# Five changes of order in one layer of a hybrid encoder: tables, scales, maxima, low halves and residual transposes

## Chip, cores and metric

The kernel runs on one core of one Trainium2 chip, in one launch. The metric is the device time of one execution in microseconds (us), the median of three runs.

## What is computed

One encoder layer over 2048 tokens of width 1024:

- h = RMSNorm(x), then one combined projection h @ w_in; its columns are q, k and v of mixer A (8 heads of 64) and the latents of mixer B (c_q of 256, c_kv of 128, a rotary key of 32).
- Mixer A is dilated sliding-window attention in three patterns, (window, stride) = (128, 1), (512, 4) and (2048, 16), with a relative bias per head; the three outputs are merged by their softmax denominators.
- Mixer B is latent attention: q = rmsnorm(c_q) @ w_q_up, keys and values = rmsnorm(c_kv) @ w_kv_up, a rotary part of 32 for q and one rotary key for all heads, and a softmax over all 2048 keys in 8 heads of 96 (values of 64).
- x = x + concat(rmsnorm(A), rmsnorm(B)) @ w_out.
- A router picks one of 4 groups of experts and 2 of 8 experts in it for each token; the gated MLPs (1024 to 256 to 1024) are added to x. A final RMSNorm follows.

```
sc = (qn . kn + qr . kr) * 96 ** -0.5       # mixer B, per head
o  = softmax(sc) @ v
x  = x + concat(rmsnorm(out_a), rmsnorm(out_b)) @ w_out
```

All inputs and outputs are float32. Where the kernel multiplies in float16 or in the rounded form of float32, it splits an operand into a high and a low part and adds three products (hi hi, hi lo, lo hi).

## The kernel before

The kernel is written as a sequence of stages, in the order in which they run: the combined projection (until about 427 us of the span), mixer A (427 to 700), the preparation of mixer B (706 to 770), its main loop (to 1515), the output projection with the router (to 1797), the experts (to about 2300) and the final norm. Every engine has its own queue and takes its instructions in the order in which the program issues them (manual_schedule, no planner); engines meet through semaphores, which follow from tiles and from the number of buffers of a pool. A tile of a pool with two buffers waits for the last reader of the tile before the last.

**Mixer A** works through 160 units (8 heads, 20 units: 4 with the table of stride 16, 8 with that of stride 1, 8 with that of stride 4). The bias tables t16, t1 and t4 are loaded once; scale_tables (L570) has POOL multiply the part of one pair of heads by a scale. For the first pair it is called ahead of the loop (L582), for the others at unit 12 of an odd head. A step s of the loop (L756) issues, in this order: the permutations of q, the scores of unit s on PE (qk), the bias and row minimum on DVE (soft1), POOL's subtraction of unit s-1 (soft2, L676), ACT's exponential of unit s-2 (soft3, L697), PE's transposes of unit s-3, and the low part and the product with v of units s-4 and s-5.

**The preparation of mixer B** (mla_prep, L1006) goes through 16 tiles c of 128 tokens: ACT normalises the latents (stage_a1, two tiles ahead); PE transposes them, ACT and DVE split them into high and low parts (stage_a2, one tile ahead); PE multiplies with the weights of q and v, DVE and POOL make the rotary part, ACT and DVE write the values VB (stage_b). qprep transposes q of head 0, put_q (ACT, DVE) writes its high and low parts Qh and Ql each fourth tile; krows and kprep make the keys of head 0. All transposes of it and krows, kprep and qk_scales take their PSUM tiles from the pool tag pT, which has two buffers. qk_scales (L793) is one small matmul and 17 operations of DVE on a few columns that set the scales of q and k; it stands ahead of stage_a2(0).

**The main loop of mixer B** (mla, L821) has 256 steps s: 8 heads, 4 blocks of 512 queries (index m counts the 32 pairs), 8 pairs of key tiles. A step issues the scores of two key tiles (6 matmuls), two exponentials of ACT (hi in float16 and p32), the low part lo = p32 - hi of the step before (lows, L920: DVE makes columns 0 to LV of each 512, POOL the rest, LV = 256), and, each second step, the products with VB of two earlier steps (pv). Two maximum passes per step (maxpass, L874: one matmul of 128 queries against 512 keys, one maximum of DVE over the row, and after the fourth of a row group a maximum over the four) are made for a block to come: they lead by 20 passes, and these 20 stand ahead of the loop, followed by mrow(0), which transposes the maxima and writes them as a row of Qh. From head 7 on, parts of the output projection are mixed into the steps (ahead5).

**The output projection** (loop over n at L1826) handles 16 tiles of 128 tokens. In an iteration n, proj(n) is a generator of the 32 matmuls and their sums, which are issued in chunks (ahead, some); between the chunks stand the work on other tiles. After chunks 1 and 2, trans(n+1) has PE transpose the merged and scaled rows ab of the next tile (8 transposes L1368, the copies to mT_hi on ACT, mT_lo on DVE). After chunks 3 and 4, trans2(n-1) has PE transpose the new residual rows x of the tile before (8 transposes, L1437), which resid(n-1) (DVE, L1395) has written after proj(n-1). Both use the pool tag pT of that stage.

Of the kernel before, what the change touches and what calls it, by code (L numbers as in the profile page):

```python
# [36 lines left out]
class K:  # L37
# [475 lines left out]
    def phase3(self):  # L513
        nc, tc, io, dr = self.nc, self.tc, self.io, self.dram
        self.pre2 = self.c_pre.enter_context(tc.tile_pool(name="p3pre2", bufs=1, side="right"))
        with ExitStack() as ctx:
# [52 lines left out]

            def scale_tables(g):  # L570
                for t in (t16, t1, t4):
                    nc.gpsimd.tensor_scalar(t[:, 2 * g:2 * g + 2], t[:, 2 * g:2 * g + 2], self.asc[:, g, 0:1], None, op0=ALU.mult)  # L572
# [8 lines left out]
            list(vl)  # L581
            scale_tables(0)  # L582

# [173 lines left out]
            for s in range(NS + 5):  # L757
                if s < NS:
                    h, u = divmod(s, U)
                    if u < 4:  # L760
                        perm_q(h, 1, u)
                    elif u < 8:
                        perm_q(h, 4, u - 4)
                    if u == 1 and h + 1 < HA:
                        self.load_qk(h + 1, q1 if h % 2 == 0 else self.pre)
                    if u == 1 and h == HA - 1:
                        self.pre4(0)
                    if u in (10, 11) and h == HA - 1:
                        self.pre4(u - 9)
                    if u in (9, 16) and h == HA - 1:  # L770
                        self.pre_b(u // 16)
                    if u == 5 and h % 2 == 0 and h // 2 + 1 < 4:
                        list(load_v(h // 2 + 1))
                    if u == 12 and h % 2 and h // 2 + 1 < 4:
                        scale_tables(h // 2 + 1)
                    qk(s)
                    soft1(s)
                if 0 <= s - 1 < NS:
                    soft2(s - 1)
                if 0 <= s - 2 < NS:  # L780
                    soft3(s - 2)
                if 0 <= s - 3 < NS:
                    trans(s - 3)
                if 0 <= s - 4 < NS:
                    low(s - 4)
                if 0 <= s - 5 < NS:
                    pv(s - 5)
                    h, u = divmod(s - 5, U)
                    if h % 2 and u in (3, 11, 19):
                        put(h // 2, {3: 16, 11: 1, 19: 4}[u])  # L790
# [30 lines left out]
    def mla(self):  # L821
        nc, tc, io, dr = self.nc, self.tc, self.io, self.dram
        LV = 256
        PASS = ((0, 0), (0, 1), (1, 0))
        with ExitStack() as ctx:
# [14 lines left out]
            vsc, vinv = self.vbs[:, 0:1], self.vbs[:, 1:2]  # L840
            sm = self.sm4 = ctx.enter_context(tc.tile_pool(name="p4sm", bufs=2))
            with ExitStack() as c2:
                self.mla_prep(c2, PASS, VB, ckvT, wkv, QK, vsc)
            self.c_pre.close()
# [5 lines left out]
            psX = ctx.enter_context(tc.tile_pool(name="p4X", bufs=1, space=PSUM))  # L850
            mz = [pp.tile([128, 4, 97], F32, name=f"mz{i}") for i in range(2)]
            for t in mz:
                nc.gpsimd.memset(t, 0.0)
            qraw, part = {}, {}

# [4 lines left out]
            def prep(h, i):  # L860
# [8 lines left out]
                else:  # L869
                    for j in range(4):  # L870
                        nc.tensor.transpose(ps[0:96, 128 * j:128 * j + 128], qraw[h][:, 4 * n4 + j], self.ident)
                    self.put_q(d, ps, sl)

            def maxpass(m, i):  # L874

                h, n = divmod(m, 4)
                d = QK[h % 2]
                qt, kc = divmod(i, 4)
                if i == 0:
                    part[m] = sm.tile([128, 4, 4], F32, name="part")  # L880
                ps = psM.tile([128, 512], F32, name="M")
                q0 = n * 512 + qt * 128
                nc.tensor.matmul(ps, d["Qh"][0:96, q0:q0 + 128], d["Kh"][0:96, kc * 512:kc * 512 + 512],  # L883
                                 start=True, stop=True)
                nc.vector.tensor_reduce(part[m][:, qt, kc:kc + 1], ps, axis=AX.X, op=ALU.max)  # L885
                if kc == 3:
                    nc.vector.tensor_reduce(mz[m % 2][:, qt, 96:97], part[m][:, qt], axis=AX.X, op=ALU.max)

# [71 lines left out]
            NM = 4 * HB  # L960
            for g in range(20):
                maxpass(g // 16, g % 16)
            mrow(0)
            NS = HB * 32
            for s in range(NS + 2):
                if s < NS:
# [5 lines left out]
                    if g < 16 * NM:  # L972
                        maxpass(g // 16, g % 16)
                    scores(s, 1)
                    if s >= 1:
                        lows(s - 1)
# [28 lines left out]

    def mla_prep(self, ctx, PASS, VB, ckvT, wkv, QK, vsc):  # L1006
        nc, tc, io, dr = self.nc, self.tc, self.io, self.dram
# [104 lines left out]
        for c in range(2):  # L1112
            stage_a1(c)
        self.qk_scales(self.sm4, pt)
        stage_a2(0)
        for c in range(NT):
            if c + 2 < NT:
                stage_a1(c + 2)
            if c + 1 < NT:
                stage_a2(c + 1)  # L1120
            stage_b(c)
            if c >= 1:
                qprep(c - 1)
            if c == 2:
                for d in QK:
# [200 lines left out]
    def phase5(self):  # L1326
# [14 lines left out]
        with ExitStack() as ctx:  # L1341
# [490 lines left out]
            for n in range(NT - 1):  # L1832
# [15 lines left out]
                some(4)  # L1848
                trans(n + 1)
                if n >= 1:  # L1850
                    resid2(n - 1)
                some(4)
# [4 lines left out]
                ahead(pj, 2)  # L1857
                if n >= 1:
                    trans2(n - 1)
                if even and n + 2 < NT:  # L1860
# [511 lines left out]
```

## Time and profile before

| | before |
|---|---|
| median of 3 runs | 2323.42 us (2323.35 to 2327.49) |
| profiled execution | 2328.61 us |
| its span | 2326.8 us |
| mean granted clock of TensorE | 0.948 |
| PE busy | 2077.9 us, 89% of the span |
| PE weight loads | 1584.7 us, 68% |
| DVE busy | 1653.5 us, 71% |
| ACT busy | 1426.9 us, 61% |
| POOL busy | 1093.3 us, 47% |
| DMA | 312.81 MB, 134 GB/s |

PE is TensorE's matmuls, PEld its weight loads, DVE is VectorE, ACT is ScalarE, POOL is GpSimd. A row of a timeline or of a group ends with the idle time of the engine ahead of it and with what released it. The granted clock is a share of full speed: 1.00 is 2.4 GHz and 0.50 is 1.2 GHz. The span in 40 equal slices, busy share in tenths:

```profile
PE   6899989688988899999999999788888899999990
...
DVE  7722221388886888888888899967787677777755
```

### The profile page before, as it was taken

What the parts mean: (1) busy time and instruction counts of PE and PEld (TensorE: products, weight loads), DVE (VectorE), ACT (ScalarE), POOL (GpSimd) and SP (SyncE); (2) the same over time, 40 slices, a digit from 0 to 9 for tenths busy, and PEclk for the clock granted to TensorE, in tenths of its full rate; (3) what the DMA queues carried; (4) which work ended last, traced back from release to release, by engine and by line L of the source; (5) the groups of instructions that cost most, each with busy time, mean ns of one, the idle gap of its engine ahead of it and who ended that gap; (6) DMA issues with size and microseconds to landing.
All of it is one profiled execution on the core that took longest, in us unless ns stands there. A gap on an engine that the chain in (4) does not pass through costs nothing. (4 is left out here: it accounts for less than half of the span.)

```text
span 2326.8 us, 42792 instructions
## 1 busy us (share of the span) xinstructions
PE 2077.9 (89%) x16087; PEld 1584.7 (68%) x16087; DVE 1653.5 (71%) x3656; ACT 1426.9 (61%) x2121; POOL 1093.3 (47%) x1193
## 2 busy tenths in 40 slices
PE   6899989688988899999999999788888899999990
PEld 5899778577777556656656555477776588788870
DVE  7722221388886888888888899967787677777755
ACT  4522211399996588888888878734443366677653
POOL 1100000278763255555555556644564656776640
PEclk9999999899998899999999999999998999999995
DMA  5412434867735100000000231145544689999978
GB/s 163 126 58 62 144 140 112 178 156 170 160 99 139 48 22 6 22 22 6 22 22 6 45 102 26 34 135 160 151 143 158 205 307 292 293 307 313 305 212 306
DMA packets 196676, 312.81 MB, mean 134 GB/s; under 512 B 64185, under 2 KB 149090, under 8 KB 183460
## 3 DMA queue, kind: packets, MB, share of 16 engines
q1 hardware_dynamic: 166420, 174.43, 26.2%
q0 software_dynamic: 29760, 134.85, 18.0%
q8 instruction: 127, 2.08, 0.4%
q10 hardware_dynamic: 288, 0.79, 0.1%
q14 instruction: 81, 0.66, 0.1%
HBM read 235.66 MB, written 101.25 MB: 145 GB/s over the span
## 5 line engine op out<-in xcount | busy, mean ns | idle before, releaser
L923 POOL TENSOR_TENSOR lo<-p,hi 128x512 f16<-128x512 f32 x256 | 342.7, 1343 | 297.3 <-ACT p L917 235.5
L916 ACT ACTIVATE hi<-S,mla_scale 128x1024 f16<-128x1024 f32 x256 | 285.2, 1114 | 136.2 <-PE S L911 134.7
L885 DVE TENSOR_REDUCE part<-M 128x1 f32<-128x512 f32 x512 | 340.4, 680 | 12.8 <-PE M L883 11.5
L917 ACT ACTIVATE p<-S,mla_scale 128x1024 f32<-128x1024 f32 x256 | 284.8, 1113 | 0.1
L922 DVE TENSOR_TENSOR lo<-p,hi 128x512 f16<-128x512 f32 x256 | 228.7, 894 | 11.3 <-ACT p L917 9.5
L945 PE MATMUL O<-VB,lo 128*128 128x65 f16 x2048 | 198.4, 194 | 7.6 <-DVE lo L922 5.3
L940 PEld LDWEIGHTS <-hi 128*128 128x128 f16 x2048 | 184.6, 98 | 28.0 <-issue 22.7
L940 PE MATMUL O<-VB,hi 128*128 128x129 f16 (+1 forms) x2048 | 198.5, 215 | 0.0
L945 PEld LDWEIGHTS <-lo 128*128 128x128 f16 x2048 | 177.5, 99 | 18.0 <-DVE lo L922 6.4
L693 POOL TENSOR_TENSOR pp<-sb,st 128x256 f32<-128x256 f32 (+1 forms) x256 | 142.6, 579 | 43.3 <-DVE st L670 30.5
L572 POOL TENSOR_SCALAR t<-t,a_scale 128x512 f32<-128x512 f32 (+1 forms) x12 | 16.1, 1351 | 305.1 <-DMA t<-d_r 290.9
L2077 DVE TENSOR_TENSOR s<-raw,s 128x1024 fp32r<-128x1024 f32 x120 | 140.2, 1221 | 15.0 <-ACT s L2075 13.8
L2121 POOL DMA_INDIRECT d_x<-o,rec x47 | 94.0, 2000 | 107.3 <-ACT s L2075 35.5
L710 PE MATMUL PT<-ident,pp 128*128 128x128 f32 (+1 forms) x640 | 104.3, 287 | 43.8 <-ACT pp L697 41.5
L2034 PE MATMUL pd<-s,hT 128*128 128x512 f32 x540 | 138.2, 404 | 1.7 <-ACT hT L2021 1.7
L1385 PE MATMUL pm<-s,mT_hi 128*128 128x512 f32 x512 | 136.1, 413 | 3.8 <-ACT mT_hi L1370 3.8
L340 DVE SCALAR_TENSOR_TENSOR qk_sb<-pm,qkscale,qk_sb 128x512 f16<-128x512 f32 x32 | 23.9, 750 | 152.5 <-ACT qk_sb L339 152.5
L697 ACT ACTIVATE pp<-pp,a_scale 128x512 f32<-128x512 f32 (+1 forms) x160 | 113.8, 711 | 29.3 <-POOL pp L687 19.8
L2075 ACT ACTIVATE s<-raw 128x1024 fp32r<-128x1024 f32 x120 | 118.3, 1050 | 11.5 <-DMA raw<-in_w_up,eidx 4.7
L2034 PEld LDWEIGHTS pd<-s,hT 128*128 128x128 f32 x540 | 101.2, 188 | 30.1 <-issue 4.3
L339 ACT ACTIVATE qk_sb<-pm,qkscale 128x512 f16<-128x512 f32 x32 | 21.9, 687 | 161.8 <-PE pm L329 110.4
L1385 PEld LDWEIGHTS pm<-s,mT_hi 128*128 128x128 f32 x512 | 98.1, 197 | 26.0 <-ACT mT_hi L1370 4.1
(502 smaller groups left out, 6081.2 us busy)
## 6 DMA issues: line engine op xcount, KB each, us to landing
x<-in_x SPq DMA_DIRECT2D x32, 512.0 KB
na<-d_na SPq DMA_DIRECT2D x48, 264.0 KB
d_qk<-qk_sb SPq DMA_DIRECT2D x64, 128.0 KB
d_x<-x SPq DMA_DIRECT2D x16, 512.0 KB
d_h<-h SPq DMA_DIRECT2D x16, 512.0 KB
y<-d_x SPq DMA_DIRECT2D x16, 512.0 KB
out<-y SPq DMA_DIRECT2D x16, 512.0 KB
d_q<-qs SPq DMA_DIRECT2D x16, 384.0 KB
```

Of the source, the lines that this page charges most:

```text
L693: nc.gpsimd.tensor_sub(dst, src, res[:, s0 + i, 65:66, None, None].to_broadcast([128, 2, na, nx // 2]))
L885: nc.vector.tensor_reduce(part[m][:, qt, kc:kc + 1], ps, axis=AX.X, op=ALU.max)
L916: nc.scalar.activation(hi, ps, AF.Exp, scale=es)
L917: nc.scalar.activation(p32, ps, AF.Exp, scale=es)
L922: nc.vector.tensor_sub(lo[:, :, 0:LV], p32[:, :, 0:LV], hi[:, :, 0:LV])
L923: nc.gpsimd.tensor_sub(lo[:, :, LV:512], p32[:, :, LV:512], hi[:, :, LV:512])
L940: nc.tensor.matmul(o[:, c0:c0 + own], hi[:, j, q], V[:, 0:own], start=(kt == 0 and qt == 0), stop=False, skip_group_check=True)
L945: nc.tensor.matmul(o[:, c0:c0 + 65], lo[:, j, q], V[:, 0:65], start=False, stop=(kt == 15 and qt == 3), skip_group_check=True)
L1385: nc.tensor.matmul(ps[half], mT[a][:, j], wo[b][j // 2][:, j % 2, 512 * half:512 * half + 512], start=(n == 0), stop=(n == 23))
L2034: self.nc.tensor.matmul(ps[:, half], hT[a][:, j], w[b][:, j, 512 * half:512 * half + 512], start=(n == 0), stop=(n == len(k) - 1))
L2075: nc.scalar.activation(hi, src, AF.Copy)
L2077: eng.tensor_sub(lo, src, hi)
```

## The change

Five edits, none of which changes what is computed:

1. At the head of mixer A only t16 is scaled ahead of the loop; t1 is scaled at step 1 and t4 at step 5, each ahead of that step's scores.
2. qk_scales moves from ahead of stage_a2(0) to behind stage_b(0).
3. Of the 20 maximum passes ahead of mixer B's loop, 12 move into its preparation, two each after tiles 5, 6, 8, 9, 12 and 13, with PSUM tiles of the tag pT; the 4 against the last 512 keys stay ahead of the loop; the 4 of block 1 go to steps 0 and 1. The clearing of mz moves ahead of the preparation.
4. LV goes from 256 to 128.
5. In the output projection trans2(n-1) and trans(n+1) trade places.

```
-            def scale_tables(g):
-                for t in (t16, t1, t4):
+            def scale_tables(g, ts):
+                for t in ts:
                     nc.gpsimd.tensor_scalar(t[:, 2 * g:2 * g + 2], t[:, 2 * g:2 * g + 2], self.asc[:, g, 0:1], None, op0=ALU.mult)
...
-            scale_tables(0)
+            scale_tables(0, (t16,))
...
-                        scale_tables(h // 2 + 1)
+                        scale_tables(h // 2 + 1, (t16, t1, t4))
+                    if s in (1, 5):
+                        scale_tables(0, (t1,) if s == 1 else (t4,))
                     qk(s)
                     soft1(s)
...
-        LV = 256
+        LV = 128
...
+            def maxpass(m, i, ps=None):
...
+                if ps is None:
+                    ps = psM.tile([128, 512], F32, name="M")
...
-            for g in range(20):
-                maxpass(g // 16, g % 16)
+            for qt in range(4):
+                maxpass(0, 4 * qt + 3)
             mrow(0)
...
                     scores(s, 1)
+                    if s < 2:
+                        maxpass(1, 2 * s)
+                        maxpass(1, 2 * s + 1)
                     if s >= 1:
                         lows(s - 1)
...
-        self.qk_scales(self.sm4, pt)
         stage_a2(0)
...
             stage_b(c)
+            if c == 0:
+                self.qk_scales(self.sm4, pt)
             if c >= 1:
                 qprep(c - 1)
+            if c >= 5 and c % 4 in (0, 1) or c == 6:
+
+                kc, half = {5: (0, 0), 6: (0, 1), 8: (1, 0), 9: (1, 1), 12: (2, 0), 13: (2, 1)}[c]
+                for qt in (2 * half, 2 * half + 1):
+                    maxpass(0, 4 * qt + kc, pt.tile([128, 4, 128], F32, name="pT").rearrange("p a b -> p (a b)"))
...
                 some(4)
-                trans(n + 1)
                 if n >= 1:
+                    trans2(n - 1)
                     resid2(n - 1)
...
                 ahead(pj, 2)
-                if n >= 1:
-                    trans2(n - 1)
+                trans(n + 1)
```

## Rows read from the trace of the kernel before

**Rows 1.** Stages: stretch, length, busy us (instructions) PE, PEld, DVE, ACT, POOL, clock, DMA, GB/s.

```profile
460.00:480.00 20.00, 19.23 (x313) 17.45 (x310) 19.67 (x92) 19.82 (x40) 16.32 (x26) 1.00 1.18 250
716.00:770.00 54.00, 53.52 (x312) 49.11 (x310) 39.91 (x118) 42.14 (x97) 22.12 (x42) 1.00 0.54 143
770.50:786.80 16.30, 11.50 (x26) 2.93 (x27) 15.16 (x28) 0.68 (x1) 0.56 (x2) 0.61 0.25 73
880.00:1340.00 460.00, 450.99 (x4595) 277.11 (x4593) 404.96 (x691) 380.63 (x400) 246.78 (x210) 1.00 0.08 20
1376.00:1424.00 48.00, 42.48 (x396) 24.68 (x395) 46.82 (x73) 32.62 (x36) 34.43 (x33) 0.93 0.25 77
1494.00:1513.00 19.00, 12.04 (x117) 7.02 (x115) 19.00 (x12) 10.78 (x11) 18.22 (x11) 0.78 0.03 8
```

**Rows 2.** POOL's timeline, head of mixer A: start, busy us, line, operation, idle before.

```profile
446.38 1.56 POOL L572 TENSOR_SCALAR t<-t,a_scale 128x512 f32<-128x512 f32 x1 [33.74 <-DMA t<-d_r]
447.90 4.06 POOL L687 TENSOR_TENSOR pp<-sb,st 128x512 f32<-128x512 f32 x4
452.16 0.98 POOL L693 TENSOR_TENSOR pp<-sb,st 128x192 f32<-128x192 f32 x2 [0.20 <-ACT QA L536]
```

**Rows 3.** ACT's timeline, the exponential of unit 4.

```profile
455.41 0.62 ACT L697 ACTIVATE pp<-pp,a_scale 128x384 f32<-128x384 f32 x1
```

**Rows 4.** PE's timeline, preparation of mixer B, tiles 0, 7 and 15.

```profile
712.48 1.01 PE L1061 MATMUL pq<-wq_hi,cqT_lo 128*128 128x384 f32 x2 [0.87 <-DVE cqT_lo L1050]
...
733.67 0.49 PE L1045 MATMUL pT<-ident,cn 128*128 128x128 f32 x3
...
762.55 0.49 PE L1045 MATMUL pT<-ident,cn 128*128 128x128 f32 x3
```

**Rows 5.** DVE's timeline, preparation of mixer B.

```profile
735.48 0.74 DVE L1080 SCALAR_TENSOR_TENSOR VB<-pv,vb_scale,VB 128x512 f16<-128x512 f32 x1
...
764.17 0.42 DVE L1050 TENSOR_TENSOR cqT_lo<-pT,cqT_hi 128x256 fp32r<-128x256 f32 x1
```

**Rows 6.** DVE's timeline, the first maxima ahead of the loop.

```profile
772.12 2.47 DVE L885 TENSOR_REDUCE part<-M 128x1 f32<-128x512 f32 x4
```

**Rows 7.** PE's timeline, the first scores of the loop.

```profile
786.79 0.58 PE L909 MATMUL S<-s,s 97*128 97x512 f16 x1 [0.98 <-DVE s L894]
```

**Rows 8.** Groups, 880 to 1340: line, busy us, mean ns, idle before.

```profile
L923 POOL TENSOR_TENSOR lo<-p,hi 128x512 f16<-128x512 f32 x168 | 223.9, 1337 | 188.4 <-ACT p L917 140.9 <-PE S L911 44.1 <-PE M L883 3.5
L922 DVE TENSOR_TENSOR lo<-p,hi 128x512 f16<-128x512 f32 x167 | 140.6, 842 | 8.7 <-ACT p L917 7.3
```

**Rows 9.** DVE's timeline, the low halves of two steps.

```profile
792.50 1.42 DVE L922 TENSOR_TENSOR lo<-p,hi 128x512 f16<-128x512 f32 x1
...
1002.79 0.69 DVE L922 TENSOR_TENSOR lo<-p,hi 128x512 f16<-128x512 f32 x1
```

**Rows 10.** POOL's timeline, the low halves of the same steps.

```profile
792.22 1.17 POOL L923 TENSOR_TENSOR lo<-p,hi 128x512 f16<-128x512 f32 x1 [21.15 <-ACT p L917]
...
1002.84 1.67 POOL L923 TENSOR_TENSOR lo<-p,hi 128x512 f16<-128x512 f32 x1 [2.79 <-ACT p L917]
```

**Rows 11.** PE's timeline, output projection, an odd and an even tile.

```profile
1601.92 0.66 PE L1368 MATMUL pT<-ident,ab 128*128 128x128 f32 x4 [2.37 <-ACT ab L1313]
...
1603.29 3.44 PE L1385 MATMUL pm<-s,mT_lo 128*128 128x512 f32 x8
...
1617.01 1.03 PE L1368 MATMUL pT<-ident,ab 128*128 128x128 f32 x8
1619.74 2.03 PE L1385 MATMUL pm<-s,mT_hi 128*128 128x512 f32 x8
...
1625.21 1.97 PE L1437 MATMUL pT<-ident,x 128*128 128x128 f32 x8 [3.44 <-DVE mT_lo L1371]
```

**Rows 12.** DVE's timeline, the residual sums of the same tiles.

```profile
1600.57 1.22 DVE L1395 TENSOR_TENSOR x<-pm,x 128x1024 f32<-128x1024 f32 x1
...
1620.20 1.21 DVE L1395 TENSOR_TENSOR x<-pm,x 128x1024 f32<-128x1024 f32 x1
```

More of the change, by code (lines that the diff above doesn't have):

```diff
@@ L841, in mla @@
             sm = self.sm4 = ctx.enter_context(tc.tile_pool(name="p4sm", bufs=2))
+            mz = [pp.tile([128, 4, 97], F32, name=f"mz{i}") for i in range(2)]
+            for t in mz:
+                nc.gpsimd.memset(t, 0.0)
+            part = {}
+            def maxpass(m, i, ps=None):
+                h, n = divmod(m, 4)
+                d = QK[h % 2]
+                qt, kc = divmod(i, 4)
+                if m not in part:
+                    part[m] = sm.tile([128, 4, 4], F32, name="part")
+                if ps is None:
+                    ps = psM.tile([128, 512], F32, name="M")
+                q0 = n * 512 + qt * 128
+                nc.tensor.matmul(ps, d["Qh"][0:96, q0:q0 + 128], d["Kh"][0:96, kc * 512:kc * 512 + 512],
+                                 start=True, stop=True)
+                nc.vector.tensor_reduce(part[m][:, qt, kc:kc + 1], ps, axis=AX.X, op=ALU.max)
+                if kc == 3:
+                    nc.vector.tensor_reduce(mz[m % 2][:, qt, 96:97], part[m][:, qt], axis=AX.X, op=ALU.max)
             with ExitStack() as c2:
-                self.mla_prep(c2, PASS, VB, ckvT, wkv, QK, vsc)
+                self.mla_prep(c2, PASS, VB, ckvT, wkv, QK, vsc, maxpass)
             self.c_pre.close()
@@ L850, in mla @@
             psX = ctx.enter_context(tc.tile_pool(name="p4X", bufs=1, space=PSUM))
[L851 to L854, printed above, removed]
+            qraw = {}
             def load_q(h):
@@ L872, in prep @@
                     self.put_q(d, ps, sl)
[L874 to L887, printed above, removed]
             def mrow(m):
@@ L1004, in put_q, with mla_prep @@
         nc.vector.scalar_tensor_tensor(d["Ql"][0:96, sl], ps[0:96], sq, d["Qh"][0:96, sl], op0=ALU.mult, op1=ALU.subtract)
-    def mla_prep(self, ctx, PASS, VB, ckvT, wkv, QK, vsc):
+    def mla_prep(self, ctx, PASS, VB, ckvT, wkv, QK, vsc, maxpass):
         nc, tc, io, dr = self.nc, self.tc, self.io, self.dram
```

## Prediction, made before the result

> **What bounds the kernel now.** I read the span table and the forty slices first: TensorE (PE) is busy 89% of the span, and the five edits sit in four stretches, so the stage table came next [rows 1]. In it the reader is to see which engine is full where. At the head of mixer A (460 to 480) ACT and DVE are full (19.82 and 19.67 of 20 us) and POOL is not (16.32). In the preparation of mixer B (716 to 770) PE is at its bound: 53.52 of 54 us at a granted clock of 1.00. In mixer B's middle (880 to 1340) PE is busy 450.99 of 460; in its loaded part (1376 to 1424) DVE is, 46.82 of 48; at its end (1494 to 1513) DVE is busy 19.00 and POOL 18.22 of 19. Then I read the queues of single engines around each edit, for what each instruction waited for, since every queue follows the order in which the program was written.
>
> **Head of mixer A (tables).** POOL scales t16, t1 and t4 in one go and waits 33.74 us, until 446.38, for t4 to land. Only after it, at 447.90, come units 0 to 3 of the subtraction, 4.06 us [rows 2]. With t1 moved to step 1 and t4 to step 5, these four stand ahead of the wait: they, and the exponentials and the scores behind them, run while t4 is on its way. Nothing on SP's queue moves, so t4 lands as before. Unit 4's subtraction (452.16 [rows 2]) still follows the t4 operation, now some 4.2 us sooner; ACT, which started unit 4's exponential at 455.41 [rows 3], finds no four units ahead of it and starts it at about 449.0, 6.4 sooner. POOL's slack at 460 to 480 lets it keep up, ACT and DVE are what binds there, so the gain lies between the two: I take -5.5 (ends -6.5 and -1; -1 if POOL behind t4 still sets the pace).
>
> **qk_scales after stage_b(0).** Seventeen small DVE instructions leave the place ahead of the first cqT_lo, for which PE waited 0.87 us [rows 4]. They now run after tile 0's VB and hold the next lows by a little: -1 (ends -2 and +1).
>
> **Twelve maxima into the preparation of mixer B.** Each is a matmul and a reduction on DVE (0.62 us: 2.47 for four [rows 6]), two of them after tiles 5, 6, 8, 9, 12 and 13, and they take tiles of the pool pT, which has two buffers. With the transposes of the next tile in buffer 0, the first maximum takes buffer 1, the second buffer 0, and the transposes after that need buffer 1 again: PE, in order, stands at them until the first reduction is done. That reduction is queued on DVE behind the rotary products and VB of the tile that PE has only just finished. After tile 13, PE reaches the place at 762.55 [rows 4], DVE is free at 764.17 [rows 5], plus 0.62 is 764.8: 2.3 us. After tile 5, 733.67 [rows 4] against 735.48 + 0.74 [rows 5] + 0.62 = 736.8: 3.2 us. The other four lie between (after 8 and 12 a Ql of DVE stands ahead too). Six times the mean of 2.75 is 16.5; the twelve matmuls run inside these waits. Since PE is the bound there, all of it is on the path. Waits also cost clock: soon after a wait of 2.37 us, eight matmuls of the output projection took 3.44 us, where the same eight took 2.03 at 1619.74; but the eight transposes after a wait of 3.44 us show no loss, at 1.97 [rows 11]. I take 0.5 of the 1.4 for each of six, +3, and for the edit **+19.5** (ends: +2.6 if the waits are hidden and only twelve matmuls of 0.22 are left, half of the 0.44 that PE's 26 instructions of 11.50 us take at 770 to 787 at a clock of 0.61 [rows 1]; +25 with the 1.4 lost at all six).
>
> **The head that becomes shorter.** The twenty maxima start at 772.12 [rows 6] and the first scores stand until 786.79 [rows 7]; DVE is busy 15.16 of the 16.3 us [rows 1]. Four are left, and sixteen times 0.62 go: -10. Four others come into steps 0 and 1, each 0.44 us of PE by the same 11.50 over 26, partly beside DVE: +1.5. Together **-8.5** (ends -11 and -7). The clearing of mz on POOL hides behind the preparation, where POOL is busy 22.12 of 54 us [rows 1].
>
> **Low halves 1:3.** DVE's operation shrinks from 512 to 256 elements a row, POOL's grows to 768. One DVE operation alone takes 0.69 (1002.79) [rows 9] and one of POOL alone 1.17 (792.22) [rows 10]; by size DVE's should be about 0.4 and POOL's 1.7, estimates. In the middle, DVE's low takes 842 ns in the mean and POOL's 1337 over 168 of them [rows 8], so each is stretched by the other. There PE is idle for only 9.0 of 460 us [rows 1]; whatever DVE gains, not more than that can come out, and I take half, -4, for the whole loop. In the loaded part, where DVE binds, a DVE operation that comes behind a longer one of POOL waits about 0.5 longer, while its own time shrinks by some 0.3; one that comes first only gains the 0.3: -1 (ends -5 and +3). At the end, where the two alternate and both are full [rows 1], the longer POOL operation is on the path: six or so steps by 0.2, and 0.5 for the last: +1.5. Together **-3.5** (ends -12 and +6).
>
> What the rows show of the two engines together: DVE's low that began at 1002.79 took 0.69 and POOL's, at 1002.84, 1.67; where POOL began first, at 792.22, it took 1.17, and DVE's at 792.50 took 1.42 [rows 9, 10]. The one that begins first has its time, the other waits for it. The Trainium skill ("SBUF — State Buffer", section "Who interferes with whom") calls the port pair that DVE shares with GpSimd an exclusive lock and not a shared bandwidth; the trace agrees. It speaks against the edit: by it a longer POOL operation makes the waits of DVE longer, and of the halved DVE time little comes back, which is about the -3.5; were it a shared bandwidth, the halved operation would cost half its 842 ns everywhere, and the loop gain the -12.
>
> **Output projection.** In odd tiles PE waits at the first place for the next tile's rows ab (2.37 us at 1601.92) [rows 11]. The residual's transposes, which now stand there, need x, and x is written by DVE from 1600.57 for 1.22 us, to 1601.79 [rows 12]: the wait stays, with another releaser. In even tiles x comes late: at 1620.20 + 1.21 = 1621.4 [rows 12], where PE reaches the place at 1617.01 [rows 11], a new wait of 4.4 us; but the 3.44 at the later place (1625.21) [rows 11] goes, as the next tile's transposes need only rows that are long ready. There are three such tiles (6, 10 and 14 are alike): 3 x 1.0 = 3.0 lost; DVE makes the same lows in either order, so part of it can come back in the next wait, and I take the middle between 3.0 and nothing: **+1.5** (ends -1 and +5).
>
> **The sum.** -5.5 - 1 + 19.5 - 8.5 - 3.5 + 1.5 = +2.5. The profiled execution took 2328.61 us (span 2326.8, 1.8 around it), 5.2 above the median of 2323.42; I take the sum as a difference and put it on the median: **2325.9 us**.
>
> **Rivals.**
> *Slower: the preparation loses its clock.* Place: 716 to 770, price: the 1.4 us of [rows 11] at all six waits and the same again in the tiles between, which are now cut short, so 2 x 6 x 1.4 less the 3 that I took = +14, of which half is likely inside the next wait: about +8, time 2334. It decides if the granted clock of the preparation is below about 0.85 (it is 1.00 now [rows 1]). For it: the 3.44 for eight matmuls. Against: the 1.97 after a longer wait [rows 11].
> *Faster: DVE's low costs half everywhere.* POOL does not hold DVE up, the loaded part and the middle both get DVE time back, and mixer B gains 12 instead of 3.5; some of the preparation's waits, where DVE is 14 us idle [rows 1], are shorter as well: 2.5 - 8.5 - 5 = -11, time 2312. For it: DVE at 46.82 of 48 in the loaded part [rows 1]. Against: PE's 9 idle us in all of the middle [rows 1], and the 1.42 behind the 1.17 [rows 9, 10].
> *The tables do not do what they say.* POOL's t4 operation stands in front of unit 4 all the same, ACT meets the same wait a few units later, and only 1 us comes back: +4.5, time 2330.5.
>
> **How the numbers follow.** A difference of 0.2%, 4.65 us, is about what a measurement of this kernel can tell from no change. The forecast, in which a loss and several gains nearly cancel, has its own range of 2319 to 2331 and a chance of 0.46: same 0.33, slower 0.11, faster 0.02. The lost clock has 0.20 (slower), the cheap low 0.25 (faster), the tables 0.06 (half slower, half same), and 0.03 is left, spread evenly. Faster 0.02 + 0.25 + 0.01 = 0.28; same 0.33 + 0.03 + 0.01 = 0.37; slower 0.11 + 0.20 + 0.03 + 0.01 = 0.35. The range takes in the bounds of the lows and most of the clock case: 2311 to 2336.
>
> **What would show it.** Tables: POOL's first subtraction at about 429 instead of 447.90 and ACT's unit 4 at about 449. Preparation: PE's transposes behind six waits of 2 to 3 us whose releaser is a maximum of DVE, and a stretch longer by 16 to 20 us. Head: the first scores about 10 us sooner after the preparation's end. Lows: POOL's near 1.7 us, DVE's near 0.4 plus waits, PE's waits for DVE in the middle gone. Projection: PE's waits in front of the residual's transposes, with x as releaser. I am wrong if the preparation is longer by less than 8 us, which would make the kernel faster, or if mixer B's middle moves by more than 5.

## The result: slower by 0.6%, and the profile after

| | before | changed |
|---|---|---|
| median, 8 runs each | 2323.58 us | 2334.61 us |
| ratio of the two | | 1.0060, 95% interval 1.0044 to 1.0075 |
| profiled execution, span | 2328.61, 2326.8 us | 2336.27, 2334.5 us |
| mean granted clock | 0.948 | 0.950 |

By the ratio that is 14 us more (10 to 17); the two medians differ by 11.0. The forecast was 2325.9 us and no measurable change; the time lies in the range, but at its upper end. One of best_a's eight executions took 4666.80 us, twice the others, and is left out of its ratio below.

The two profiled executions differ by 7.7 us only, so I did not sum differences between these two. Five of the kernels below (only_swap, next_late, resid_soon, swap_next_soon, swap_resid_late) share all code ahead of the output projection with the kernel before; the six profiles give a mean for each stage (standard deviation 0.0 to 0.3 us, 1.1 in the last row). Step 208 lies just ahead of step 210, from which on parts of the output projection are mixed into the steps. Against this mean, in us:

| stage, by landmarks | mean | forecast | changed | undo_max | early_max | only_low | best_a |
|---|---|---|---|---|---|---|---|
| t4 scaled, to the exponential of unit 20 | 30.8 | -5.5 | -5.9 | -4.8 | -6.0 | 0.0 | -5.8 |
| preparation of B, transposes of tile 0 to 4 | 14.7 | -1 | -1.0 | -1.0 | -0.8 | +0.6 | -0.9 |
| transposes of tile 4, to the last of q | 47.4 | +19.5 | +20.9 | -0.1 | +13.4 | -0.1 | -0.1 |
| to the first scores | 16.4 | -10 | -10.0 | +0.1 | -9.4 | +0.2 | +0.2 |
| head 0 | 89.7 | +1.5 | +3.3 | -0.3 | +3.4 | -0.7 | -0.3 |
| head 1 to step 208 | 486.2 | -4 | -6.1 | -6.1 | -6.2 | -6.1 | -6.1 |
| step 208 to the last product with VB | 150.3 | +0.5 | +6.3 | +10.1 | +10.1 | +6.3 | +1.7 |

The profile of undo_swap, whose code is that of the changed kernel up to the output projection, repeats the changed column within 0.2 us, but for the third row: +17.9. The last row is less steady than its deviation says. Its mean is five profiles of 149.5 to 149.9 and the 152.7 of the kernel before; with LV = 128 to the end it took 156.5 or 156.6 in three profiles (changed, undo_swap, only_low) and 160.4 in two (undo_max, early_max), though their code there is the same.

In the output projection the three profiles with the swap (changed, undo_max, only_swap) stand against five with the old order (before, undo_swap, early_max, only_low, best_a). From the last product with VB to the first sum x: 26.1 against 22.2. From there to the sum x of tile 14: 238.7 (238.5 to 238.9) against 234.8 (233.0 to 236.3). Together **+7.8**, where +1.5 was forecast. The column of the changed kernel and this add up to +15.3, near the 14 that the ratio gives and more than the 11 between the medians; the stretch from unit 20 to the preparation, which is not in the table, is 1.9 shorter than its mean.

The five with the old order are not one group. From the last product with VB to the sum x of tile 14 the two with LV = 256 at the end took 255.5 (before) and 254.5 (best_a), the three with LV = 128 took 258.8 (undo_swap), 258.5 (only_low) and 257.8 (early_max). So some 3 us of the longer output projection go with the lows 1:3 ahead of it. Of the 9.3 us by which the changed kernel (264.8) exceeds the kernel before here, 6.0 go with the swap (264.8 - 258.8) and 3.3 with these lows.

**Tables.** POOL's timeline of the changed kernel, then ACT's. The reader is to see that the four subtractions now stand ahead of the wait for t4, and that unit 4's follow right behind t4's scaling, at the head of the row of eight [rows 2, 3].

```profile
427.23 4.07 POOL L687 TENSOR_TENSOR pp<-sb,st 128x512 f32<-128x512 f32 x4 [16.56 <-ACT QA L533]
444.74 1.56 POOL L572 TENSOR_SCALAR t<-t,a_scale 128x512 f32<-128x512 f32 x1 [13.44 <-DMA t<-d_r]
446.27 4.39 POOL L693 TENSOR_TENSOR pp<-sb,st 128x192 f32<-128x192 f32 x8
```

```profile
447.27 0.61 ACT L697 ACTIVATE pp<-pp,a_scale 128x384 f32<-128x384 f32 x1 [12.60 <-POOL pp L693]
```

**Preparation of mixer B.** The stage of the changed kernel by windows (columns as in [rows 1]), then the queues of PE and DVE. PE's busy share falls from nearly all to 55.24 of 68.23 us; its transposes stand behind a maximum of DVE, here at three of the six places (1.75, 2.50 and 1.86 us, ahead of tiles 7, 14 and 15). DVE's two reductions come behind VB and, here, Ql.

```profile
711.58:779.81 68.23, 55.24 (x286) 48.17 (x284) 43.16 (x117) 38.12 (x84) 20.62 (x38) 0.92 0.39 104
```

```profile
725.05 0.52 PE L1053 MATMUL pT<-ident,cn 128*128 128x128 f32 x3 [1.75 <-DVE part L861]
...
764.70 0.60 PE L1053 MATMUL pT<-ident,cn 128*128 128x128 f32 x3 [2.50 <-DVE part L861]
...
766.38 0.84 PE L1069 MATMUL pq<-wq_hi,cqT_lo 128*128 128x384 f32 x2
...
771.97 0.52 PE L1053 MATMUL pT<-ident,cn 128*128 128x128 f32 x3 [1.86 <-DVE part L861]
```

```profile
762.56 0.75 DVE L1088 SCALAR_TENSOR_TENSOR VB<-pv,vb_scale,VB 128x512 f16<-128x512 f32 x1
763.22 0.74 DVE L1012 SCALAR_TENSOR_TENSOR s<-xq,mla_scale,s 96x512 f16<-96x512 f32 x1
763.88 1.27 DVE L861 TENSOR_REDUCE part<-pT 128x1 f32<-128x512 f32 x2
```

**Low halves.** Groups of the changed kernel from 880 to 1340 [rows 8]: POOL's low takes 1732 ns, DVE's 724 for half the columns, and PE's waits for DVE's maxima are gone. The first line is the kernel before, where the same group of PE waited 3.2 us for them.

```profile
L883 PE MATMUL M<-Kh,Qh 96*128 96x512 f16 x168 | 63.4, 377 | 3.9 <-DVE part L885 3.2
```

```profile
L928 POOL TENSOR_TENSOR lo<-p,hi 128x768 f16<-128x768 f32 x169 | 291.2, 1732 | 122.6 <-ACT p L922 71.4 <-PE S L916 36.7 <-PE M L859 13.2
L927 DVE TENSOR_TENSOR lo<-p,hi 128x256 f16<-128x256 f32 x169 | 122.4, 724 | 5.0 <-ACT p L922 4.3
L859 PE MATMUL M<-Kh,Qh 96*128 96x512 f16 x172 | 64.9, 377 | 1.4
```

From step 208 on the same groups say something else: first the kernel before (1362 to 1505), then the changed one (1359 to 1506). DVE's low is half as large and takes 1082 instead of 1100 ns, POOL's 1772 instead of 1361, and PE's waits for DVE's maxima grow from 11.7 to 15.8 us in this group. The 1100 is the highest of six: from 1357 to 1500 the five other kernels with the old lows have 1028 to 1089 ns, so the halved operation gains nothing that is clear of the scatter.

```profile
L923 POOL TENSOR_TENSOR lo<-p,hi 128x512 f16<-128x512 f32 x47 | 63.8, 1361 | 41.5 <-ACT p L917 38.7 <-PE S L911 1.5 <-DVE part L885 1.2
L922 DVE TENSOR_TENSOR lo<-p,hi 128x512 f16<-128x512 f32 x45 | 49.5, 1100 | 0.6 <-ACT p L917 0.5
L883 PE MATMUL M<-Kh,Qh 96*128 96x512 f16 x64 | 24.9, 388 | 12.1 <-DVE part L885 11.7
```

```profile
L928 POOL TENSOR_TENSOR lo<-p,hi 128x768 f16<-128x768 f32 x46 | 81.3, 1772 | 28.8 <-ACT p L922 25.4 <-PE M L859 2.3 <-PE S L916 1.1
L927 DVE TENSOR_TENSOR lo<-p,hi 128x256 f16<-128x256 f32 x47 | 50.8, 1082 | 0.5 <-ACT p L922 0.2
L859 PE MATMUL M<-Kh,Qh 96*128 96x512 f16 x64 | 24.1, 377 | 16.2 <-DVE part L861 15.8
```

**Output projection.** PE's timeline of the changed kernel, around tiles 1, 6 and 7: it waits for x at the first place in even tiles, as forecast (4.29), and also 3.91 and 3.16 in odd tiles, where 0.34 + 0.30 and 0.52 + 0.30 stood before. The first two lines are the kernel before at tiles 1 and 7.

```profile
1538.75 0.66 PE L1368 MATMUL pT<-ident,ab 128*128 128x128 f32 x4 [0.34 <-ACT ab L1313]
...
1639.26 0.66 PE L1368 MATMUL pT<-ident,ab 128*128 128x128 f32 x4 [0.52 <-ACT ab L1313]
```

```profile
1543.21 1.97 PE L1451 MATMUL pT<-ident,x 128*128 128x128 f32 x8 [3.91 <-DVE x L1409]
...
1623.39 1.97 PE L1451 MATMUL pT<-ident,x 128*128 128x128 f32 x8 [4.29 <-DVE x L1409]
...
1630.45 1.03 PE L1382 MATMUL pT<-ident,ab 128*128 128x128 f32 x8
...
1644.48 1.09 PE L1451 MATMUL pT<-ident,x 128*128 128x128 f32 x8 [3.16 <-DVE x L1409]
```

DVE's timeline shows what the sum x is queued behind: DVE is idle for 8.39 and 3.53 us ahead of the lows of tiles 1 and 7, which PE's transposes feed one place later than before. The first two lines are the kernel before, where DVE was idle for 4.52 us ahead of the same lows of tile 1 and not at all ahead of those of tile 7.

```profile
1527.45 1.29 DVE L1371 TENSOR_TENSOR mT_lo<-pT,mT_hi 128x512 fp32r<-128x512 f32 x2 [4.52 <-ACT mT_hi L1370]
...
1624.48 1.27 DVE L1371 TENSOR_TENSOR mT_lo<-pT,mT_hi 128x512 fp32r<-128x512 f32 x2
```

```profile
1532.04 1.29 DVE L1385 TENSOR_TENSOR mT_lo<-pT,mT_hi 128x512 fp32r<-128x512 f32 x2 [8.39 <-ACT mT_hi L1384]
...
1631.71 1.29 DVE L1385 TENSOR_TENSOR mT_lo<-pT,mT_hi 128x512 fp32r<-128x512 f32 x2 [3.53 <-ACT mT_hi L1384]
...
1643.20 1.22 DVE L1409 TENSOR_TENSOR x<-pm,x 128x1024 f32<-128x1024 f32 x1
```

### The profile page after: what moved, and what is told of

Same layout as the page of the kernel before. It is cut to its first block, busy times and chain, and to the rows that moved or that the text cites. A ratio compares the mean times of both kernels' runs of the same rounds, so it can differ in the third digit from the quotient of the medians.

```text
span 2334.5 us, 42766 instructions
## 1 busy us (share of the span) xinstructions
PE 2077.7 (89%) x16087; PEld 1585.2 (68%) x16087; DVE 1632.3 (70%) x3656; ACT 1427.9 (61%) x2121; POOL 1195.9 (51%) x1193
## 3 DMA queue, kind: packets, MB, share of 16 engines
q0 software_dynamic: 29760, 134.85, 17.9%
## 5 line engine op out<-in xcount | busy, mean ns | idle before, releaser
L928 POOL TENSOR_TENSOR lo<-p,hi 128x768 f16<-128x768 f32 x256 | 443.4, 1740 | 197.6 <-ACT p L922 130.3
L861 DVE TENSOR_REDUCE part<-M 128x1 f32<-128x512 f32 x500 | 332.8, 679 | 16.9 <-PE M L859 15.8
L927 DVE TENSOR_TENSOR lo<-p,hi 128x256 f16<-128x256 f32 x256 | 205.1, 802 | 7.0 <-ACT p L922 5.9
L693 POOL TENSOR_TENSOR pp<-sb,st 128x256 f32<-128x256 f32 (+1 forms) x256 | 142.5, 580 | 38.7 <-DVE st L670 26.1
L2134 POOL DMA_INDIRECT d_x<-o,rec x47 | 94.7, 2016 | 105.1 <-ACT s L2088 41.2
L339 ACT ACTIVATE qk_sb<-pm,qkscale 128x512 f16<-128x512 f32 x32 | 21.9, 687 | 162.1 <-PE pm L329 115.0
```

The costliest lines, as they stand in the source:

```text
L693: nc.gpsimd.tensor_sub(dst, src, res[:, s0 + i, 65:66, None, None].to_broadcast([128, 2, na, nx // 2]))
L927: nc.vector.tensor_sub(lo[:, :, 0:LV], p32[:, :, 0:LV], hi[:, :, 0:LV])
L928: nc.gpsimd.tensor_sub(lo[:, :, LV:512], p32[:, :, LV:512], hi[:, :, LV:512])
```

## The experiments

Four runs asked which of the two suspected parts (the swap and the maxima in the preparation) costs the time, and by which mechanism. Times below are medians; ratios stand against the kernel before, whose median was 2322.31 us beside these four.

**undo_swap.** The changed kernel, the output projection as before:

```
-                    trans2(n - 1)          # after chunk 2
+                trans(n + 1)
...
-                trans(n + 1)               # after chunk 4
+                    trans2(n - 1)
```

> The changed kernel with the two kinds of transposes of the output projection back in their old places. Theory (ping-pong): the swap costs 9 us, because the lows of the next tile, now later in DVE's queue, hold DVE idle and so make x late, for which PE waits: this kernel takes about 5 us more than the kernel before (2328 to 2330 against 2323.6), and the output projection is as long as before within 2 us. Rival (the swap only trades one wait for another, +1.5, as forecast, and the stretch is longer from what came ahead of it, the lows 1:3 or the clock): still 11 to 13 us more than before, with the output projection 7 us longer than before.

2330.96 us, ratio 1.0042 (1.0027 to 1.0057): 9.8 us over before by the ratio, 8.7 by the medians, between the two expectations. The stretch from the last product with VB to the sum x of tile 14 is 258.8 us, against 264.8 with the swap and 255.5 in the profile of before. The swap costs some 4 us by the ratios and 6 by this stretch, and more than I thought is left to other parts; 3.3 us of it stand in the output projection itself, with the old order.

**undo_max.** The changed kernel, all 20 passes ahead of the loop and none in the preparation or in steps 0 and 1:

```
-            for qt in range(4):
-                maxpass(0, 4 * qt + 3)
+            for g in range(20):
+                maxpass(g // 16, g % 16)
...
```

> The changed kernel with all 20 maximum passes ahead of mixer B's loop again. Theory (buffer wait): the twelve maxima cost about 20 us in the preparation and give back about 6 in the head and the first steps, so this kernel is some 14 us faster than the changed one and level with the kernel before (2321 to 2326). Rival (the preparation's waits are made up later, since the loop starts with a lead): only 5 us faster than the changed one, 2330 to 2333.

2326.97 us, ratio 1.0014 (1.0002 to 1.0027). Against the changed kernel that is 11 us by the ratios (0.46%) and 7.6 by the medians, between the two expectations; its preparation is 47.3 us, the mean. By the three stages that the passes touch the loss is 20.9 - 10.0 + 3.3 = 14.2. The rival, a loss made up later, does not fit: behind head 0 the changed kernel has the stages of only_low (-6.1 and +6.3). But in this profile the stage from step 208 on is 3.8 longer than in the changed kernel, with the same code, and that takes part of the 14.2 back; why is open.

**only_swap.** The kernel before with the swap alone.

> The kernel before with nothing but the swap in the output projection. Theory (ping-pong): 8 to 10 us slower than before, 2332 to 2334, all of it between 1515 and 1800. Rival (one wait for another): 1 to 2 us slower, 2325.

2327.93 us, ratio 1.0026 (1.0015 to 1.0037): +6.0 us (3.5 to 8.6), between the two expectations. In its trace the loss stands in the output projection, 264.4 us where the kernel before has 255.5. The forecast's +1.5 is out.

**early_max.** undo_swap, eleven maxima one per tile and ahead of that tile's products, the old places in the preparation empty:

```
                 stage_a2(c + 1)
+            if c >= 5:
+                i = c - 5
+                maxpass(0, 4 * (i % 4) + i // 4, pt.tile(...))
             stage_b(c)
...
```

> The changed kernel with the old places in the output projection, and the maxima of the preparation put elsewhere: one per tile for tiles 5 to 15 (eleven), issued between the next tile's transposes and this tile's products, so that each reduction stands ahead of the rotary products and VB in DVE's queue and no pT buffer is asked for while its reduction is still queued; the twelfth goes back ahead of the loop. Theory (buffer wait behind DVE's queue): the six waits go, only eleven matmuls of 0.22 to 0.4 us are added to the preparation (+2.5 to +4.5), and the kernel is 12 to 16 us faster than the one with only the swap undone: about 2313 to 2317. Rival (the preparation has no room on DVE or loses its clock wherever the maxima stand): within 5 us of the one with only the swap undone, about 2325 to 2329.

2324.30 us, ratio 1.0009 (0.9998 to 1.0021): 7 to 8 us faster than undo_swap, half of what the theory said and just outside the rival's range. The trace shows why. PE's timeline of this kernel, then DVE's: the maximum in the turn of tile 5, behind the transposes of tile 6, waits 2.27 us for its buffer, which the key rows made in the turn of tile 4 used last, and whose low is queued on DVE behind VB and Ql. There are six such waits, four behind key rows (7.8 us) and two behind the keys of kprep (2.4 us).

```profile
719.84 0.38 PE L859 MATMUL pT<-s,s 96*128 96x512 f16 x1 [2.27 <-DVE s L1101]
```

```profile
717.61 0.74 DVE L1089 SCALAR_TENSOR_TENSOR VB<-pv,vb_scale,VB 128x512 f16<-128x512 f32 x1
718.27 0.74 DVE L1013 SCALAR_TENSOR_TENSOR s<-xq,mla_scale,s 96x512 f16<-96x512 f32 x1
719.04 0.75 DVE L1101 SCALAR_TENSOR_TENSOR s<-pT,mla_scale,s 32x512 f16<-32x512 f32 x1
```

These waits are 10.2 of the preparation's +13.4 us; the rest, some 3, is the eleven matmuls, at a granted clock of 1.00. So what costs most is the wait for the buffer, not the maximum. It was tested again in best_c.

The next four took the swap apart, one chunk of eight matmuls at a time, and the lows by themselves. The kernel before took 2320.48 us beside them.

**next_late.** The kernel before; the next tile's transposes after chunk 3:

```
-                trans(n + 1)
...
-                ahead(pj, 2)
+                ahead(pj, 1)
+                trans(n + 1)
+                ahead(pj, 1)
                     trans2(n - 1)
```

> The kernel before, with the transposes of the next tile one chunk of eight matmuls later (after chunk 3 instead of 2); the residual's stay after chunk 4. Theory (DVE's queue): the lows of the next tile stand in DVE's queue ahead of the next sum x; one chunk of 1.9 us later they hold DVE idle in the even tiles, about a third of the swap's cost comes: 2 to 4 us slower than before, the output projection longer by as much. Rival (the swap costs only by the wait for x at the first place): no loss, rather 2 to 5 us gained, since the waits of PE for the rows ab in odd tiles (2.4 to 6.2 us) get one chunk of cover.

2316.48 us, ratio 0.9978 (0.9965 to 0.9991): 5 us faster, as the rival had it. My theory in this form falls: lows that come a chunk later do not cost by themselves. The sum x of tile 0 is 1.1 us late, as the theory has it, but from the next tile on that is more than made up.

**resid_soon.** The kernel before; the residual's transposes after chunk 3:

```
-                ahead(pj, 2)
+                ahead(pj, 1)
                     trans2(n - 1)
+                ahead(pj, 1)
```

> The kernel before, with the residual's transposes one chunk of eight matmuls sooner (after chunk 3 instead of 4); the next tile's stay after chunk 2. Theory (DVE's queue): no lows of the next tile move, x comes as soon as before; only waits for x of up to 2 us in tiles where it is late, and these are there already: within 2 us of before. Rival (the wait for x at the first place is the cost): about half of the swap's cost, 3 us slower.

2312.18 us, ratio 0.9967 (0.9951 to 0.9983): 7.7 us faster. Neither theory had that, and the rival (x asked for too early) had the wrong sign.

**only_low.** LV = 128 alone.

> The kernel before with LV = 128 alone. Theory from the traces so far (gains in the unloaded heads, loses in the loaded ones): one us less per head in heads 1 to 6, and 3 to 9 us more between 1360 and 1515, so within 3 us of before, 2320 to 2326. Rival (the low halves 1:3 gain as forecast): 3.5 us faster or more, and no loss after 1360.

2323.50 us, ratio 1.0011 (0.9999 to 1.0022): no gain, as the theory had it. In its trace 6.1 us are gained between head 1 and step 208 and 6.3 lost after it, as in the changed kernel, and the output projection is 3.0 us longer than that of the kernel before.

**best_a.** Tables, qk_scales, and the lows 1:3 only where they gain:

```
+                LV = 128 if s < 208 else 256
```

> The kernel before with three of the five edits: the tables, qk_scales, and LV = 128 only in the steps below 208 (before the output projection's work is mixed in), 256 after. Theory: -6 from the tables, -1 from qk_scales, -6 from six heads: 10 to 13 us faster than before, 2310 to 2313. Rival (gains at the head of mixer A are given back at the joints of the stages): 4 to 7 us faster.

2310.68 us, ratio 0.9959 (0.9938 to 0.9979): 9.5 us faster (5 to 14). The stage after step 208 is back at +1.7 and the output projection at 254.5 us, so both losses went with the split 1:3 in the steps from 208 on.

By then the cause of the swap's cost was open, so the last four asked again. Beside them the kernel before took 2321.36 us.

**swap_next_soon.** The residual's transposes after chunk 2, the next tile's after chunk 3 (one chunk sooner than in the change).

> The kernel before with half of the swap taken back: the residual's transposes after chunk 2 (as in the change), the next tile's after chunk 3 (the change: 4, before: 2). Theory (DVE's queue: the next tile's lows, late, make the next x late): DVE's idle time ahead of these lows shrinks by one chunk of 1.9 us, most of the swap's 5.6 us goes, 0 to 3 us slower than before. Rival (x is asked for too early, whatever stands behind it): still 4 to 7 us slower, PE waiting for x 2 us or more in most tiles.

2313.75 us, ratio 0.9968 (0.9953 to 0.9984): 7.4 us faster than before, although PE asks for x as early as in the change and still waits 17.7 us for it in nine tiles (31.1 in the change). The rival falls, and the theory, which had 0 to 3 us slower, has missed as well.

**swap_resid_late.** The residual's transposes after chunk 3, the next tile's after chunk 4.

> The kernel before with the other half of the swap taken back: the next tile's transposes after chunk 4 (as in the change), the residual's one chunk ahead of them, after chunk 3 (the change: 2, before: 4). Theory (DVE's queue): the lows of the next tile are as late as in the change and x with them; 3 to 7 us slower than before. Rival (x asked for too early): x has one chunk more, the waits for it go, and the time is that of the two moves by one chunk that were measured, 3 to 8 us faster than before.

2316.79 us, ratio 0.9988 (0.9975 to 1.0001): 3 us faster or the same, at the edge of what the rival had. The lows of the next tile are as late as in the change (the first sum x comes 26.0 us after the last product with VB, as with the swap; 22.3 before), and the cost is gone all the same.

Put together, the order matters little where one chunk lies between the two places (0.3 and 2.3 us) and more where two do (6.0); how far apart the places stand matters in both orders. Times are differences to the kernel before; the waits are DVE's, ahead of the lows of both kinds of transposes, from the sum x of tile 0 to that of tile 14, and the length is that of this stretch:

| places (chunks) | next tile first | DVE waits, length | residual first | DVE waits, length |
|---|---|---|---|---|
| 2 and 4 | before: 0 | 28.6, 233.2 | only_swap: +6.0 | 37.9, 238.5 |
| 2 and 3 | resid_soon: -7.7 | 13.1, 225.0 | swap_next_soon: -7.4 | 12.0, 223.1 |
| 3 and 4 | next_late: -5.1 | 14.0, 227.4 | swap_resid_late: -2.8 | 13.7, 227.4 |

The length goes with DVE's waits. All of them together, not those ahead of the lows alone, are 41.2 us before and 45.9 in only_swap, 35.8 in resid_soon and 33.6 in swap_next_soon, 37.2 in next_late and 37.6 in swap_resid_late; the length less these is 189 to 193 us in all six. This is an account and not yet a cause: DVE is busy about 183 to 186 us of the stretch in every variant, so whatever makes it longer shows as idle time of DVE. PE's account differs. With the swap its waits grow by 6.6 us (from 24.7, 15.0 for ab and 9.7 for mT_lo, to 31.3), about as much as the length does (5.3). But from the kernel before to swap_next_soon, which is 10 us shorter, they fall only to 21.9 (17.7 for x, 4.2 for hT); the other 7 us are time outside of these waits, at a mean granted clock of 0.98 there, 0.95 before and 0.93 with the swap. How much of the length the clock sets and how much DVE's waits, no run here separates.

DVE's waits, first in the kernel before, then in the changed one, then in swap_next_soon (columns: what waits for what, us in total, times, longest):

```profile
DVE hT L1444 <- ACT hT L1443: 20.6, 12, 3.3
DVE mT_lo L1371 <- ACT mT_hi L1370: 8.0, 7, 2.5
```

```profile
DVE mT_lo L1385 <- ACT mT_hi L1384: 31.9, 13, 4.0
DVE hT L1458 <- ACT hT L1457: 6.4, 6, 2.5
```

```profile
DVE nm L1287 <- POOL na L1282: 12.9, 4, 5.7
DVE h L1426 <- POOL nw L1256: 7.7, 5, 3.8
DVE hT L1444 <- ACT hT L1443: 6.5, 6, 2.5
DVE mT_lo L1371 <- ACT mT_hi L1370: 5.5, 10, 1.0
```

With two chunks between the places, whichever lows stand at the later place take the larger wait (20.6 of hT before, 31.9 of mT_lo in the change). With one chunk the waits ahead of the lows are half or less, but part of that comes back at other instructions: DVE's waits for POOL (nm and h) are 10.6 us before and 20.6 in swap_next_soon.

**best_b.** best_a with the residual's transposes after chunk 3.

> Tables, qk_scales and the low halves 1:3 below step 208, with the residual's transposes one chunk sooner (after chunk 3). Theory (the two gains stand in different stages and add): -10 and -8, 2300 to 2306 where the kernel before takes about 2322. Rival (the gain of the earlier transposes was the sum of chances of phase in that stretch and depends on when it starts): 2308 to 2312, as without it.

2297.39 us, ratio 0.9897 (0.9876 to 0.9917): 24 us faster than before (19 to 29), more than the 17 that the two gave by themselves and below the range that the theory had.

**best_c.** best_b with five maxima in the preparation, at tiles whose buffer is free:

```
+        early = {6: 0, 10: 1, 13: 2, 14: 6, 15: 10}
...
+            if c in early:
+                maxpass(0, early[c], pt.tile(...))
             stage_b(c)
```

> The same, with five of the twelve maxima of block 0 in the preparation of mixer B, at the five tiles (6, 10, 13, 14, 15) where the PSUM buffer that they take was last used by transposes whose lows are done, ahead of that tile's products. Theory (a maximum costs the preparation only when its buffer still waits for DVE): the preparation is at most 2 us longer and the head 3 us shorter, so 0 to 3 us faster than without them. Rival (each maximum costs PE or DVE time in the preparation wherever it stands): 2 to 6 us slower.

2295.20 us, ratio 0.9886 (0.9866 to 0.9906). In time it can't be told from best_b; in the trace the preparation is 1.4 us longer than the mean, at a granted clock of 1.00, and the stage up to the first scores 3.3 shorter, as the theory had it. PE's timeline shows the maximum without a wait, in an unbroken row:

```profile
741.91 0.49 PE L1051 MATMUL pT<-ident,cn 128*128 128x128 f32 x3
742.40 0.39 PE L858 MATMUL pT<-s,s 96*128 96x512 f16 x1
742.44 0.70 PE L1067 MATMUL pq<-wq_hi,cqT_hi 128*128 128x384 f32 x2
```

It is the fastest kernel here, 26 us (22 to 31) below the kernel before and some 40 below the changed one.

## Why the prediction was wrong

The sum was +2.5 and the stages show +15.3; the time shows 11 to 14. Term by term:

- **Tables, -5.5, shown: -5.9.** The step from POOL's queue to ACT's was right, and neither end of the range came.
- **qk_scales, -1, shown: -1.0.**
- **Maxima in the preparation, +19.5, shown: +20.9** (+17.9 in undo_swap's profile). Six waits of 1.7 to 2.5 us in the place that was named, with the releaser that was named, are 12.0 us in sum. PE's busy time grows by 8.8 (55.24 against 46.41 in undo_max). Of that some 3.6 are the twelve matmuls, an estimate from early_max, whose eleven add 3.3 at a clock of 1.00 (49.72 against 46.41); the other 5 go with the clock: the stage's granted clock is 0.92, and pairs of matmuls that take 0.51 at full clock took 0.84 at 766. In undo_swap the waits are the same (12.2) and the clock is 0.97; so the 3 us between the two profiles are clock as well. The forecast counted its 16.5 from PE's arrival, with the matmuls inside; against it stand 12.0 + 3.6 = 15.6. The clock cost more than the 3 taken, and the row that spoke against it was misread: eight transposes "show no loss, at 1.97", but eight such transposes take 1.03 at 1617.01 [rows 11], and the granted clock from 1625.2 to 1627.1 was 0.50. The rival of the lost clock needed less than 0.85; it was right in kind, and not the largest miss.
- **Head, -10 and +1.5, shown: -10.0 and +3.3.** The first steps run at a clock of 0.50 from 786 to 796 (0.78 in the first 10 us of the loop before), and the four passes stand in them. Their matmuls had been priced at 0.44 each, but PE also waits there for their reductions, 0.35 us at 790.57 and 0.36 at 795.35, and the scores between them run at the lower clock as well.
- **Low halves, -3.5, shown: about +3** (-6.1 and +6.3, and some +3 in the output projection, which the +7.8 below holds in part; only_low by itself took 3 us longer, -0.2 to +5). The middle gained 6.1 where 4 was taken, which is more than the 5 that the prediction named as a sign of being wrong, though it helps the kernel. The term that failed is the loaded part and the end: "a DVE operation that comes behind a longer one of POOL waits about 0.5 longer, while its own time shrinks by some 0.3 ... -1" and +1.5. Shown is +6.3. DVE is busy 147.0 of the 156.6 us of this stage (143.2 of 152.7 before), and half the columns did not make its low shorter: 1082 ns, where the old lows have 1028 to 1100. The loss of 3 behind it, in a stretch whose code the edit does not touch, was in no term. The Trainium skill ("SBUF — State Buffer", section "Who interferes with whom") says that a DVE instruction with two SBUF inputs contends with a GpSimd instruction that reads SBUF, and that the port pair which they share is an exclusive lock. These means agree with it. The cheap low of the second rival falls by them: in the middle too, half the columns brought the low only from 842 to 724 ns. I had weighed the wait behind POOL and then let a gain of 0.3 stand beside it that did not come.
- **Output projection, +1.5, shown: +7.8 in the traces, of which the swap is 6.0, and +6.0 in time by itself (only_swap).** This is the step that failed most. Its even tiles came as said (4.29 for 4.4). The failing sentence is "DVE makes the same lows in either order, so part of it can come back in the next wait": the accounting was of PE's waits alone. DVE takes its queue in order too, and the lows that I moved hold it idle until PE's later place (8.39 us at tile 1, 3.53 at tile 7); everything behind them, x among it, comes later, and PE then waits in odd tiles too (3.91 and 3.16 us), where the forecast left the wait as it was. My first account of that, lows late and so x late, was too narrow as well: next_late has these lows one chunk later than before and swap_resid_late as late as the change, and neither loses. What is shown is that the cost goes with two chunks between the places in the new order, and that DVE's waits grow with it; the cause stays open.

Not settled: why two chunks between the places cost DVE more waiting than one in each pair of tiles, and what part of it is the clock; I have the waits by line, not a step by step account. Also open is why the output projection of the old order is some 3 us longer behind lows of 1:3 (258.8, 258.5 and 257.8 against 255.5 and 254.5). From the first sum x on, the mean granted clock there is 0.92 and 0.93 in these three and 0.95 and 0.96 in the other two, which is a trace of it and not shown to be its cause.

## What to carry to other kernels

When two engines feed each other through queues that run in order, moving one step moves it in every queue that it issues to: write down the idle time of the consumer ahead of its own instructions, not only the waits of the busiest engine. Before an instruction is put into a stage that an engine fills, follow its PSUM buffer, not only its time: ask who used it last and what stands ahead of that reader. And split a term by the stages that bind differently: the same edit gained 6 us where PE was full and lost 6 where DVE nearly was, and 3 more behind it; using it in the first alone kept the gain.

## What was not expected of the hardware

The time at which t4 lands ranged from 440.7 to 448.3 us in fourteen profiles whose loads up to there are the same, about as much as the effect that was to be measured; only differences of stages between landmarks, over several profiles, told the parts apart. And the same code does not always take the same time inside a stage: with the same lows the stage from step 208 on came out at 149.5 to 149.9 us five times and at 152.7 once, or at 156.5 to 156.6 three times and at 160.4 twice.
